# Two first loads and the end of VectorE's work tied in program order, and seven chunks of the last product held for its own PSUM banks

## The chip, the cores and the metric

The kernel runs on one core of one Trainium2 chip. The metric is the device time of one execution in microseconds (us), the median of several runs. Engines are named as in the profile: PE is TensorE's matmuls and PEld its weight loads, DVE is VectorE, ACT is ScalarE, POOL is GpSimd and SP is SyncE. A letter q behind an engine's name (SPq) stands for that engine's sequencer, which also issues DMAs.

## The reference

One layer of a decoder trunk on 256 tokens with 2048 features, all in float32. Only its last part is touched by the end of the change:

```python
h = rms_norm(x, norm_ffn_pre)
a, b = jnp.split(h @ w_up, 2, axis=-1)            # w_up: 2048 x 11264
c = conv_b + sum(conv_w[j] * shifted(a, j))       # width 3, causal
y = (gelu(c, approximate=True) * b) @ w_down      # w_down: 5632 x 2048
x = x + rms_norm(y, norm_ffn_post)                # out: 256 x 2048
```

Before it stand a norm, one combined projection `w_in`, two kinds of attention (latent and sliding-window), their output products, two sigmoid gates and `w_out`.

## The kernel before

**Weights.** Every weight comes from HBM in chunks of 128 rows by 1024 columns (512 KB, float32), by a DMA on SP's queue into a `raw` tile. `convert` (L157, L158) splits a chunk in two: ScalarE's CAST rounds it to `whi`, VectorE's subtraction leaves the rest in `wlo`. A product then takes three matmuls for each 128 x 512 piece, high by high, high by low and low by high (`mm3`, L189 to L191, or L500 for the first product), so one chunk with both halves of the tokens (t = 0 and t = 1, 128 tokens each) makes 12 matmuls of 512 columns. VectorE's and ScalarE's part of a chunk runs some chunks ahead of TensorE, as far as the rings of `raw` and `whi`/`wlo` tiles allow.

**Start.** SP loads `gx` and the `xr` tiles (the columns of x) and chunks of `w_in` in turn. The first product (L500 for the first four rows of chunks, L189 to L191 for the rest) has the banks `acckv` and `accq`. The chunk `raw_201` feeds 12 matmuls, then `raw_224`, `raw_245` and `raw_268` feed 12 each.

**Two tiles that are free from the start.** `raw_x` (tag `rx`, in the pool `base`) is one more raw tile that `new_raw` deals out in turns in the FFN's part; its first user is the chunk `raw_8782` of `w_up`. The staging tile of `park_sums` (tag `sg`; its loads are L234) takes two chunks of `w_down`; VectorE subtracts them from one another there (L238) and POOL's queue writes the results to DRAM (L243, L248), from where the seven-product steps below load them. Its first user is `tc_s`, in the middle of the attention. A scheduler places an instruction where it thinks that it can start; the first loads into these two tiles wait for nothing that was written before. `tc.keep_in_program_order` ties an instruction to its place among the others of its engine.

**The last product.** `w_down` is multiplied in column blocks of 1024. The last one, named `dc`, has the rows from 24 x 128 on and the columns from 1024 on. Its four PSUM banks are `cdc`: c[0] and c[1] for t = 0 (columns 1024 to 1535 and 1536 to 2047), c[2] and c[3] for t = 1. `pair_gemm` goes through the order "ppsspssppp": p (`plain`) is two chunks with 12 matmuls each; s (`seven_parked`) is two chunks' worth in seven products instead of eight, with parked sums and four more banks `qdc`. In the last six chunks only t = 0 is multiplied as they come (6 matmuls a chunk); the operands of t = 1 are kept in the list `held`, and are multiplied behind them (`rest`) into four new banks `zb`. So c[0] and c[1] are whole earlier, and the norm of t = 0 runs beside the matmuls of t = 1. The first of the held chunks is converted into two tiles of its own (`wh`), since the ring's would be reused.

**The end on VectorE.** `z_block` adds a bank to the sum so far (`ds`, L1387), ScalarE squares the result with a running sum, and VectorE multiplies by the gain `gpost` (L1390). `z_pre` (L1406 to L1408) gathers the sums of all but the last 256 columns; `finish` makes the scale `rz` (L1413 on ScalarE, L1414 to L1418 on VectorE), and its four `result` steps (L1422) make 512 columns of the output each, whose DMA (L1425) follows on SP's queue. Before, what c[2] and c[3] hold is added by L1478, what the banks `zb` hold by L1387 and L1489, and the last two `result` steps of t = 0 are kept behind the last `z_block` of t = 1.

**x2b.** The residual stream is loaded again for the last step by `unpark` (L1256, four DMAs of 256 KB for each t) into the memory of the token sums `sb`, so each of these loads waits until TensorE has read the last of those sums.

Of the kernel before, what the change touches and what calls it, by code (L numbers as in the profile page):

```python
# [11 lines left out]
F32 = mybir.dt.float32  # L12
F32R = mybir.dt.float32r
# [3 lines left out]
ALU = mybir.AluOpType  # L17
AX = mybir.AxisListType

P = 128  # L20
# [22 lines left out]
def trunk_layer(ctx, tc, x, x_cols_in, conv_cols_in, g_mix_post, g_ffn_post, w_in, w_q, w_kv,  # L43
                sinks, rel, wo_a, wo_b, w_out, w_up, w_down, rope_tab, strip_sel, out):
    nc = tc.nc
# [14 lines left out]
    def sb(pl, shape, name, dt=F32, tag=None, bufs=None):  # L60
        return pl.tile(shape, dt, name=name, tag=tag or name, **({"bufs": bufs} if bufs else {}))
# [55 lines left out]
    more_raw = []  # L117
# [10 lines left out]
    def wchunk(src, shape, own=None, rawp=None, rbufs=1, parts=None):  # L128
        i = cnt[0]
        cnt[0] += 1  # L130
        n = int(np.prod(shape))
        raw = rawp.tile([P, 1024], F32, name=f"raw{i}", tag="xraw", bufs=rbufs) if rawp else \
            new_raw(f"raw{i}")
        dst = raw[:, :n]
        if len(shape) == 2:
            dst = dst.rearrange("p (a b) -> p a b", a=shape[0])
        elif len(shape) == 3:
            dst = dst.rearrange("p (a b c) -> p a b c", a=shape[0], b=shape[1])
        if len(shape) == 3:
            for k in range(shape[0]):  # L140
                nc.sync.dma_start(dst[:, k], src[:, k])
        else:
            nc.sync.dma_start(dst, src)
        return convert(raw, n, own=own, parts=parts)

    def convert(raw, n, own=None, parts=None, into=None):
# [14 lines left out]
    def raw_row(src, n=1024):  # L161
        i = cnt[0]
        cnt[0] += 1
        raw = new_raw(f"raw{i}")
        nc.sync.dma_start(raw[:, :n], src)
        return raw

    steps = defaultdict(list)
# [19 lines left out]
    def mm3(o, ah, al, bh, bl, start, stop):  # L188
        pe.matmul(o, ah, bh, start=start, stop=False)  # L189
        pe.matmul(o, ah, bl, start=False, stop=False)  # L190
        pe.matmul(o, al, bh, start=False, stop=stop)  # L191
# [27 lines left out]
    def weight_sums(even, odd, ta, tb):  # L219
# [3 lines left out]
        vec.tensor_tensor(tb[:, a], odd[:, b], ta[:, a], op=ALU.subtract)  # L223
        vec.tensor_tensor(tb[:, b], odd[:, a], tb[:, a], op=ALU.subtract)

    def park_sums(name, w, k, c0, pl, tag, t0, bufs=None):

        td = [dram.tile([P, 1024], F32, name=f"{name}{i}") for i in range(2)]
        st = []

        def load():
            st.append(sb(pl, [P, D], f"{name}s", tag=tag, bufs=bufs))
            for i in range(2):
                pool.dma_start(st[0][:, i * 1024:(i + 1) * 1024], w[(k + i) * P:(k + i + 1) * P, c0:c0 + 1024])  # L234

        def less(o, x, y):
            o, x, y = (st[0][:, i * 512:(i + 1) * 512] for i in (o, x, y))
            tc.keep_in_program_order(vec.tensor_tensor(o, x, y, op=ALU.subtract))  # L238
# [12 lines left out]
        at(t0, even)  # L251
        at(t0 + 1, odd)
        return td
# [5 lines left out]
    def pair_gemm(name, w, k0, c0, order, act_of, s_of, kind, d, place=None, sums=None, parked=None, held=None, into=None):  # L259
# [13 lines left out]
        def plain(u, last):  # L273
            for k in (2 * u, 2 * u + 1):
                chunks[0] -= 1
                w_ = convert(raw_row(row(k)), 1024, into=into() if hold and chunks[0] == hold - 1 else None)
                for t in range(NT):
                    if t and chunks[0] < hold:
                        held[hold - 1 - chunks[0]] = (act_of(k, 1), w_)
                        continue  # L280
                    for j in range(2):
                        mul(c[2 * t + j], act_of(k, t), half(w_, j),
                            chunks[0] == (hold if t else 0) and (j == 1 or not left[0]))
                tick()

        def seven_parked(u, last):
            s1, s2, s3, s4 = s_of(u)
            if not q:
                q[:] = banks(1 - kind, f"q{name}_")
            q1, q5, q7, q6 = q  # L290
            w_ = convert(raw_row(row(2 * u + 1)), 1024)
            mul(c11, act_of(2 * u + 1, 0), half(w_, 0))
            mul(c12, s4, half(w_, 1))
            w_ = convert(raw_row(row(2 * u)[:, 0:512], 512), 512)
            mul(q1, act_of(2 * u, 0), half(w_, 0), last)
# [7 lines left out]
            mul(c21, act_of(2 * u + 1, 1), half(w_, 0), last and 0 < hold == chunks[0])  # L303
            tick()
            if last:
                end_sums()
# [1072 lines left out]

    ssz = [sb(p3, [P, NB], f"ssz{t}") for t in range(NT)]  # L1380

    def z_block(acc, b, t, later=None):
# [4 lines left out]
        vec.tensor_tensor(z, zo, acc[:, o:o + n], op=ALU.add)  # L1387
        jt = sb(p6, [P, 512], f"zj{b}_{t}", tag="jk", bufs=1)
        act.activation(jt[:, :n], z, AF.Square, accum_out=ssz[t][:, b:b + 1])
        scaled = lambda: vec.tensor_tensor(zo, z, gpost2[c0 // 1024][:, c0 % 1024:c0 % 1024 + n], op=ALU.mult)  # L1390
        if later is None:
            scaled()
        elif callable(later):
            later()
            scaled()
        else:
            at(later, scaled)
# [12 lines left out]
    def finish(t, late=()):  # L1410
# [6 lines left out]
        vec.scalar_tensor_tensor(w, v, y[:, 0:1], y, op0=ALU.mult, op1=ALU.mult)  # L1417
        vec.scalar_tensor_tensor(r, w, 1.5, y, op0=ALU.add, op1=ALU.mult)  # L1418

        def result(j):  # L1420
            a, b = 512 * j, 512 * j + 512
            ins = vec.scalar_tensor_tensor(dsum_all[t][:, a:b], dsum_all[t][:, a:b], r[:, 0:1], x2_all[t][:, a:b], op0=ALU.mult, op1=ALU.add)  # L1422
            if j in late:
                tc.keep_in_program_order(ins)
            nc.sync.dma_start(out[t * P:(t + 1) * P, a:b], dsum_all[t][:, a:b])  # L1425

        for j in range(4):
            if j not in late:
                result(j)
        return lambda: [result(j) for j in late]  # L1430
# [39 lines left out]
    c = pair_gemm("dc", w_down, 24, 1024, B2_ORDER, lambda k, t: (GH(k)[:, t * P:(t + 1) * P], GL(k)[:, t * P:(t + 1) * P]),  # L1470
                  lambda u: sb_of[u], 1, ud2_tiles, parked=parked_b2, held=held,
                  into=lambda: [sb(base, [P, 1024], f"wh{k}", F32R, tag=f"ahl{k}") for k in (6, 7)])
# [8 lines left out]
    def rest(o, todo, a, b):  # L1481
        o = o[:, a % 512:a % 512 + b - a]
        for i, (x_, (wh, wl)) in enumerate(todo):
            mm3(o, *x_, wh[:, a:b], wl[:, a:b], i == 0, i == len(todo) - 1)

    rest(part[0], held, 0, 512)
    z_block(part[0], 2, 1)
    rest(part[1], held[:-3], 512, 1024)
    vec.tensor_tensor(dsum[1][3], dsum[1][3], part[1], op=ALU.add)  # L1489
    for i in range(2):  # L1490
        rest(part[2 + i], held[-3:], 512 + i * 256, 768 + i * 256)
# [94 lines left out]
```

## Time and profile before

| what | us |
|---|---|
| median of 3 runs | 1464.42 (1462.93 to 1465.0) |
| the profiled execution | 1465.17 |
| its span, first to last instruction | 1463.2 |
| TensorE busy with matmuls | 1449.8 |
| VectorE busy | 1142.1 |
| ScalarE busy | 861.4 |

All times of instructions are microseconds from the start of the profiled execution's span; that execution took 1.97 us more than its span. A row of the timeline has the start, the time to the end of the last of its instructions, engine, line, operation, names of the tiles written and read, count, and in brackets the idle time before it with what ended it. A matmul's row shows its latency too (0.39 us at 512 columns); how often the array takes one is read from the distance of two starts.

### The profile page before, as it was taken

Reading aid. Unit: us, or ns where it says so; the run is one execution under the profiler, and the core shown is the slowest. Engines: PE = TensorE matmul, PEld = TensorE weight load, DVE = VectorE, ACT = ScalarE, POOL = GpSimd, SP = SyncE. Lnnn points to the kernel's source line nnn. Section 1 sums busy time; section 2 is a strip of 40 time slices with the busy share of each in tenths; the row PEclk is TensorE's granted clock in tenths of the full one; section 3 lists DMA queues with packets and bytes.
Section 4 is the critical chain, followed back from the end, with each engine's and each line's share of the span. In section 5 each row is a group of like instructions: output and inputs, shape, how many; then the busy total and the mean of one; then the engine's idle time right before and its main releaser. Section 6 shows DMA issues by size and latency. Waiting matters only on the chain.

```text
span 1463.2 us, 21340 instructions
## 1 busy us (share of the span) xinstructions
PE 1449.8 (99%) x7531; PEld 1236.5 (85%) x7531; DVE 1142.1 (78%) x1992; ACT 861.4 (59%) x1412; POOL 107.2 (7%) x192
## 2 busy tenths in 40 slices
PE   9999999999999999999999999999999999999997
PEld 7888888888888888888888888888888888888885
DVE  7688896765868765768799989776778797876798
ACT  6588875544555554446576665655646565665663
POOL 0021110010000101100000011000000100000000
PEclk9999999999999999999999999999999999999999
DMA  9756476698775779865666899756888888667875
GB/s 330 214 155 177 114 247 188 216 314 285 239 214 180 231 239 327 280 195 172 215 216 206 276 311 298 262 172 211 312 275 265 308 271 288 193 189 237 309 262 205
DMA packets 164199, 351.08 MB, mean 240 GB/s; under 512 B 20555, under 2 KB 31724, under 8 KB 164092
## 3 DMA queue, kind: packets, MB, share of 16 engines
q1 hardware_dynamic: 144480, 280.40, 59.3%
q0 software_dynamic: 19520, 69.27, 13.9%
q8 instruction: 59, 0.97, 0.3%
q14 instruction: 48, 0.39, 0.1%
q10 hardware_dynamic: 92, 0.05, 0.0%
HBM read 318.16 MB, written 31.51 MB: 239 GB/s over the span
## 4 chain that ended last, share of the span: by engine, by line
PE 93%; DVE 2%; DMA 2%; ACT 1%; issue 1%; DVEq 0%; SPq 0%; ACTq 0%
PE accg L189 11%; PE accg L191 11%; PE accg L190 11%; PE ua L1282 10%; PE ub L1282 10%; PE ub L1286 5%; PE ua L1286 5%; PE cd L190 2%; PE cd L191 2%; PE cd L189 2%; DMA raw<-in_ffn_w_down_dram 1%; DVE wlo L158 1%; PE mpo L966 1%; PE cg L190 1%; PE cg L189 1%; PE cw L191 1%
## 5 line engine op out<-in xcount | busy, mean ns | idle before, releaser
L158 DVE TENSOR_TENSOR wlo<-raw,whi 128x1024 fp32r<-128x1024 f32 (+2 forms) x499 | 589.0, 1190 | 213.3 <-ACT whi L157 204.5
L157 ACT CAST whi<-raw 128x1024 fp32r<-128x1024 f32 (+2 forms) x499 | 508.3, 1026 | 397.9 <-PE accg L191 153.2
L189 PE MATMUL accg<-whi,ahl 128*128 128x512 f32 (+1 forms) x416 | 162.8, 391 | 0.0
L191 PE MATMUL accg<-whi,ahl 128*128 128x512 f32 (+1 forms) x416 | 160.6, 386 | 0.0
L190 PE MATMUL accg<-wlo,ahl 128*128 128x512 f32 (+1 forms) x416 | 159.8, 384 | 0.0
L1282 PE MATMUL ub<-ahl,whi 128*128 128x512 f32 x640 | 154.6, 391 | 0.0
L1282 PE MATMUL ua<-ahl,whi 128*128 128x512 f32 x640 | 154.6, 391 | 0.0
L1282 PEld LDWEIGHTS ua<-ahl,whi 128*128 128x128 f32 x640 | 117.5, 188 | 22.7
L1282 PEld LDWEIGHTS ub<-ahl,whi 128*128 128x128 f32 x640 | 117.5, 188 | 22.6
L189 PE MATMUL accg<-whi,bhl 128*128 128x512 f32 x320 | 125.6, 393 | 0.0
L191 PE MATMUL accg<-whi,bhl 128*128 128x512 f32 x320 | 124.8, 390 | 0.0
L190 PE MATMUL accg<-wlo,bhl 128*128 128x512 f32 x320 | 124.7, 390 | 0.0
L191 PEld LDWEIGHTS accg<-whi,ahl 128*128 128x128 f32 x416 | 78.1, 188 | 15.5
L190 PEld LDWEIGHTS accg<-wlo,ahl 128*128 128x128 f32 x416 | 78.2, 188 | 13.1
L189 PEld LDWEIGHTS accg<-whi,ahl 128*128 128x128 f32 x416 | 78.2, 188 | 12.9
L1286 PEld LDWEIGHTS ub<-ahl,wlo 128*128 128x128 f32 x640 | 82.2, 191 | 3.2
L1286 PEld LDWEIGHTS ua<-ahl,wlo 128*128 128x128 f32 x640 | 82.2, 191 | 3.1
L1286 PE MATMUL ua<-ahl,wlo 128*128 128x256 f32 x640 | 83.7, 283 | 0.0
L1286 PE MATMUL ub<-ahl,wlo 128*128 128x256 f32 x640 | 83.3, 283 | 0.0
L191 PEld LDWEIGHTS accg<-whi,bhl 128*128 128x128 f32 x320 | 60.1, 188 | 12.6
L189 PEld LDWEIGHTS accg<-whi,bhl 128*128 128x128 f32 x320 | 60.1, 188 | 12.1
L190 PEld LDWEIGHTS accg<-wlo,bhl 128*128 128x128 f32 x320 | 60.1, 188 | 12.1
(624 smaller groups left out, 2535.9 us busy)
## 6 DMA issues: line engine op xcount, KB each, us to landing
raw<-in_ffn_w_up_dram SPq DMA_DIRECT2D x142, 512.0 KB, 4.7
raw<-in_w_in_dram SPq DMA_DIRECT2D x105, 512.0 KB, 4.6
raw<-in_ffn_w_down_dram SPq DMA_DIRECT2D x66, 512.0 KB, 5.5
xraw<-in_ffn_w_up_dram SPq DMA_DIRECT2D x34, 512.0 KB, 5.5
raw<-in_w_o_swa_dram SPq DMA_DIRECT2D x32, 512.0 KB, 5.0
raw<-in_w_o_mla_dram SPq DMA_DIRECT2D x32, 512.0 KB, 5.2
raw<-in_w_out_dram SPq DMA_DIRECT2D x26, 512.0 KB, 4.4
ta_s<-in_ffn_w_down_dram POOLq DMA_DIRECT2D x24, 512.0 KB, 6.0
```

The lines of the kernel that those rows point to most:

```text
L157: act.copy(hi[:, a:b], raw[:, a:b])
L158: vec.tensor_tensor(lo[:, a:b], raw[:, a:b], hi[:, a:b].bitcast(F32), op=ALU.subtract)
L189: pe.matmul(o, ah, bh, start=start, stop=False)
L190: pe.matmul(o, ah, bl, start=False, stop=False)
L191: pe.matmul(o, al, bh, start=False, stop=stop)
L966: pe.matmul(o, w(t), p_[:, c], start=n == 0, stop=n == 5)
L1282: pe.matmul(acc[i], hi[:, c], hn[p][:, j * 512:(j + 1) * 512], start=p + j == 0, stop=stop)
L1286: pe.matmul(acc[i][:, 0:256], lo[:, c], hn[p][:, j * 512:j * 512 + 256], start=False, stop=False)
```

## The change

Four edits go together.

First, the first load into the tile `rx` is kept in program order on SP's queue (in `wchunk` or `raw_row`, whichever comes first), and the first two loads into the staging tile are kept in program order on POOL's.

Second, seven chunks are held instead of six. The seventh from the end is the second chunk of the third p, ahead of two s steps; it is converted into two tiles of its own, `wfa` and `wfb` (tag `f`), by a new `held_into`. The one after it keeps `wh`.

Third, the held matmuls of t = 1 go on in c[2] and c[3] themselves (`more=True`: the bank isn't started anew), but for the last three chunks' share of the last 512 columns, which keeps two banks `zb` of 256 columns each. The two additions L1478 and the two of the banks `zb` become one for c[2] (in `z_block`) and one for c[3].

Fourth, VectorE's order at the end: `finish(0, 2)` makes two results of t = 0, then the addition of c[2] is kept in its place, then come the other two results of t = 0, then the addition of c[3], kept in its place too, and then the two blocks of 256 columns.

```diff
+            ins = nc.sync.dma_start(dst, src)
+            if more_raw and more_raw[-1] is raw_x and "rx" not in staged:
+                staged.add("rx")
+                tc.keep_in_program_order(ins)
...
-                pool.dma_start(st[0][:, i * 1024:(i + 1) * 1024], w[(k + i) * P:(k + i + 1) * P, c0:c0 + 1024])
+                ins = pool.dma_start(st[0][:, i * 1024:(i + 1) * 1024], w[(k + i) * P:(k + i + 1) * P, c0:c0 + 1024])
+                if tag not in staged:
+                    tc.keep_in_program_order(ins)
+            staged.add(tag)
...
-    held = [None] * 6
+    held = [None] * 7
...
+    def held_into(left):
+        if left == 6:
+            return [sb(p6, [P, 1024], f"wf{n}", F32R, tag="f" + n, bufs=2) for n in "ab"]
+        if left == 5:
+            return [sb(base, [P, 1024], f"wh{k}", F32R, tag=f"ahl{k}") for k in (6, 7)]
...
-    for j in range(2):
-        vec.tensor_tensor(dsum[1][2 + j], dsum[1][2 + j], c[2 + j], op=ALU.add)
-    part = [pacc.tile([P, 512], F32, name=f"zb{i}", tag="acc") for i in range(4)]
+    part = [pacc.tile([P, 512], F32, name=f"zb{i}", tag="acc") for i in range(2)]
...
-    rest(part[0], held, 0, 512)
-    z_block(part[0], 2, 1)
-    rest(part[1], held[:-3], 512, 1024)
-    vec.tensor_tensor(dsum[1][3], dsum[1][3], part[1], op=ALU.add)
+    rest(c[2], held, 0, 512, True)
+    rest(c[3], held[:-3], 512, 1024, True)
...
-    rest_of_0 = finish(0, (2, 3))
-    z_block(part[2], 3, 1)
+    result_of_0 = finish(0, 2)
+    z_block(c[2], 2, 1, tied=True)
+    for j in (2, 3):
+        result_of_0(j)
+    tc.keep_in_program_order(vec.tensor_tensor(dsum[1][3], dsum[1][3], c[3], op=ALU.add))
+    z_block(part[0], 3, 1)
     z_pre(1)
-    z_block(part[3], 4, 1, rest_of_0)
+    z_block(part[1], 4, 1)
     finish(1)
```

How instructions stand on the engines is shown at three places. On SP's queue at the start of the program there stood before (`raw_8782` is the chunk of `w_up` in the tile `rx`):

```order
L421 DMA xr_128<-in_x_cols_dram 128x256
L143 DMA raw_201<-in_w_in_dram 128x2x512
L421 DMA xr_129<-in_x_cols_dram 128x256
L143 DMA raw_8782<-in_ffn_w_up_dram 128x2x512
L143 DMA raw_224<-in_w_in_dram 128x2x512
L421 DMA xr_130<-in_x_cols_dram 128x256
L143 DMA raw_245<-in_w_in_dram 128x2x512
```

and there stands now:

```order
L432 DMA xr_128<-in_x_cols_dram 128x256
L143 DMA raw_201<-in_w_in_dram 128x2x512
L432 DMA xr_129<-in_x_cols_dram 128x256
L143 DMA raw_224<-in_w_in_dram 128x2x512
L432 DMA xr_130<-in_x_cols_dram 128x256
L143 DMA raw_245<-in_w_in_dram 128x2x512
```

The load of `raw_8782` has left the start; it now stands behind that of `raw_8760`, its neighbour in the FFN. On POOL's queue the two loads of `tc_s` have moved from the row behind the copy of `gmat`, near the start, to the row ahead of their own write-back in the attention, behind the writes of `yb_d`. Elsewhere up to the last product no engine's order differs.

On SP's queue at the end of the program there stood before:

```order
L165 DMA raw_14270<-in_ffn_w_down_dram 128x1024
L165 DMA raw_14286<-in_ffn_w_down_dram 128x1024
L165 DMA raw_14303<-in_ffn_w_down_dram 128x1024
L1256 DMA x2b_14250<-x_d 128x512 x4
L165 DMA raw_14315<-in_ffn_w_down_dram 128x1024
L1425 DMA out_dram<-ds_7715 128x512 x4
```

and there stands now (the chunks are the same ones, with numbers 6 lower):

```order
L168 DMA raw_14264<-in_ffn_w_down_dram 128x1024
L168 DMA raw_14280<-in_ffn_w_down_dram 128x1024
L1267 DMA x2b_14244<-x_d 128x512 x4
L168 DMA raw_14297<-in_ffn_w_down_dram 128x1024
L168 DMA raw_14309<-in_ffn_w_down_dram 128x1024
L1433 DMA out_dram<-ds_7715 128x512 x4
```

Both of the last two chunks, not only the last, now stand behind the four loads of `x2b` for t = 1.

On VectorE at the end there stood before (`ds_7715` is t = 0, `ds_7716` is t = 1):

```order
L1417 SCALAR_TENSOR_TENSOR wz_14402<-vz_14400,yz_14401 128x1
L1489 TENSOR_TENSOR ds_7716<-ds_7716,zb_14347 128x512
L1390 TENSOR_TENSOR ds_7716<-ds_7716,gpost_1_13437 128x512
L1418 SCALAR_TENSOR_TENSOR rz_14403<-wz_14402,yz_14401 128x1
L1387 TENSOR_TENSOR z_1_14413<-ds_7716,zb_14348 128x256
L1422 SCALAR_TENSOR_TENSOR ds_7715<-ds_7715,rz_14403,x2b_14121 128x512 x2
L1390 TENSOR_TENSOR ds_7716<-z_1_14413,gpost_1_13437 128x256
L1406 TENSOR_REDUCE zpre_13434<-ssz_13432 128x1
L1387 TENSOR_TENSOR z_1_14421<-ds_7716,zb_14349 128x256
L1407 TENSOR_SCALAR zpre_13434<-zpre_13434 128x1
L1422 SCALAR_TENSOR_TENSOR ds_7715<-ds_7715,rz_14403,x2b_14121 128x512
```

and there stands now:

```order
L1427 SCALAR_TENSOR_TENSOR wz_14393<-vz_14391,yz_14392 128x1
L1428 SCALAR_TENSOR_TENSOR rz_14394<-wz_14393,yz_14392 128x1
L1432 SCALAR_TENSOR_TENSOR ds_7715<-ds_7715,rz_14394,x2b_14121 128x512 x2
L1398 TENSOR_TENSOR ds_7716<-ds_7716,cdc_13919 128x512
L1432 SCALAR_TENSOR_TENSOR ds_7715<-ds_7715,rz_14394,x2b_14121 128x512 x2
L1403 TENSOR_TENSOR ds_7716<-ds_7716,gpost_1_13437 128x512
L1506 TENSOR_TENSOR ds_7716<-ds_7716,cdc_13920 128x512
L1398 TENSOR_TENSOR z_1_14413<-ds_7716,zb_14338 128x256
L1398 TENSOR_TENSOR z_1_14421<-ds_7716,zb_14339 128x256
L1403 TENSOR_TENSOR ds_7716<-z_1_14413,gpost_1_13437 128x256
L1416 TENSOR_REDUCE zpre_13434<-ssz_13432 128x1
```

All four results of t = 0 now stand ahead of the last two blocks of t = 1; before, two stood among and behind them. Further up on VectorE, the additions L1474 and L352 of the seven products now stand ahead of the conversion of `raw_14249`, the fifth chunk from the end, where they stood behind it.

More of the change, by code (lines that the diff above doesn't have):

```diff
@@ L164, in raw_row @@
         raw = new_raw(f"raw{i}")
-        nc.sync.dma_start(raw[:, :n], src)
+        ins = nc.sync.dma_start(raw[:, :n], src)
+        if more_raw and more_raw[-1] is raw_x and "rx" not in staged:
+            staged.add("rx")
+            tc.keep_in_program_order(ins)
         return raw
@@ L275, in plain @@
                 chunks[0] -= 1
-                w_ = convert(raw_row(row(k)), 1024, into=into() if hold and chunks[0] == hold - 1 else None)
+                w_ = convert(raw_row(row(k)), 1024, into=into(chunks[0]) if hold else None)
                 for t in range(NT):
@@ L282, in plain @@
                         mul(c[2 * t + j], act_of(k, t), half(w_, j),
-                            chunks[0] == (hold if t else 0) and (j == 1 or not left[0]))
+                            not (chunks[0] or (t and hold)) and (j == 1 or not left[0]))
                 tick()
@@ L302, in seven_parked @@
             mul(q6, s2, half(w_, 1), last)
-            mul(c21, act_of(2 * u + 1, 1), half(w_, 0), last and 0 < hold == chunks[0])
+            mul(c21, act_of(2 * u + 1, 1), half(w_, 0))
             tick()
@@ L1380, in trunk_layer, with z_block @@
     ssz = [sb(p3, [P, NB], f"ssz{t}") for t in range(NT)]
-    def z_block(acc, b, t, later=None):
+    def z_block(acc, b, t, later=None, tied=False):
         c0, n = blocks[b]
@@ L1421, in result @@
             a, b = 512 * j, 512 * j + 512
-            ins = vec.scalar_tensor_tensor(dsum_all[t][:, a:b], dsum_all[t][:, a:b], r[:, 0:1], x2_all[t][:, a:b], op0=ALU.mult, op1=ALU.add)
-            if j in late:
-                tc.keep_in_program_order(ins)
+            vec.scalar_tensor_tensor(dsum_all[t][:, a:b], dsum_all[t][:, a:b], r[:, 0:1], x2_all[t][:, a:b], op0=ALU.mult, op1=ALU.add)
             nc.sync.dma_start(out[t * P:(t + 1) * P, a:b], dsum_all[t][:, a:b])
[L1427 to L1430, printed above, removed]
+        for j in range(n):
+            result(j)
+        return result
     a_tile = lambda name, k: sb(base, [P, 1024], name, tag=f"ahl{k}")
```

20 lines of the change are left out of this document (10 added, 10 removed).

## The prediction

> **What bounds the kernel now.** First the page: the busy times, then the chain that ended last.
>
> ```profile
> PE 1449.8 (99%) x7531; PEld 1236.5 (85%) x7531; DVE 1142.1 (78%) x1992; ACT 861.4 (59%) x1412; POOL 107.2 (7%) x192
> PE 93%; DVE 2%; DMA 2%; ACT 1%; issue 1%; DVEq 0%; SPq 0%; ACTq 0%
> ```
>
> TensorE is the bound, and the change takes no matmul away (7340 rows on that engine in both programs). So it can only win where TensorE stands or runs slowly, and behind its last matmul. The change touches the start and the end, so I cut both into stretches. The start, with TensorE's timeline:
>
> ```profile
> 13.00:14.70 1.70, 0.04 (x1) 0.00 (x0) 0.02 (x1) 1.09 (x2) 0.00 (x0) 1.00 1.06 407
> 16.40:19.80 3.40, 3.40 (x10) 2.62 (x9) 3.33 (x5) 3.33 (x8) 0.00 (x0) 0.50 1.03 390
> 19.80:22.30 2.50, 2.50 (x13) 2.02 (x12) 1.95 (x4) 2.42 (x4) 0.00 (x0) 1.00 1.05 402
> ...
> 8.01 1.81 PE L500 MATMUL accq<-whi,ahl 128*128 128x512 f32 x4
> 10.13 1.08 PE L500 MATMUL acckv<-whi,ahl 128*128 128x512 f32 x4
> 14.71 1.19 PE L500 MATMUL acckv<-whi,ahl 128*128 128x512 f32 x4 [1.67 <-ACT whi L157]
> 15.96 0.87 PE L500 MATMUL acckv<-wlo,ahl 128*128 128x512 f32 x2
> 22.26 0.39 PE L189 MATMUL acckv<-whi,ahl 128*128 128x512 f32 x1
> 24.98 0.39 PE L189 MATMUL acckv<-whi,ahl 128*128 128x512 f32 x1
> ```
>
> TensorE stands from 13.0 to 14.7 for the high half of `raw_224`, then for its low half until 15.96. From 16.4 to 19.8 its granted clock is 0.50. From 22.26 to 24.98 it makes the 12 matmuls of `raw_268`, one every 0.227 us (2.72 us a chunk), and goes on so without a gap. Why `raw_224` is late:
>
> ```profile
> 5.99 0.38 SPq L143 DMA_DIRECT2D raw<-in_w_in_dram  x1
> 13.61 1.05 ACT L157 CAST whi<-raw 128x1024 fp32r<-128x1024 f32 x1 [4.47 <-DMA raw<-in_w_in_dram]
> q1 hardware_dynamic: 751, 1.25, 57.1%
> q0 software_dynamic: 288, 1.05, 45.3%
> raw<-in_ffn_w_up_dram SPq DMA_DIRECT2D x1, 512.0 KB, 8.6
> 3.34 1.21 POOL L234 DMA_DIRECT2D tc_s<-in_ffn_w_down_dram  x2
> raw<-in_w_in_dram SPq DMA_DIRECT2D x105, 512.0 KB, 4.6
> DMA to landing us min/median/max: 3.4/7.5/8.8
> ```
>
> The load is issued at 5.99 and needs 7.6 us. The two queue rows are for 6 to 12.5 us: the transfer engines are full, and 1.05 MB of the 2.30 MB is POOL's queue, which holds only `tc_s` there. On SP's queue the 0.52 MB of `w_up` stand ahead of `raw_224`. `tc_s` is first read at 380 us, the `w_up` chunk at 855 us (rows below). So 1.57 MB that nobody needs yet pass in front of what TensorE waits for: at the 390 to 407 GB/s of the stretches above 3.9 to 4.0 us of transfer.
>
> **First edit, the two ties.** Without those bytes `raw_224` needs at most the 4.6 us that is the median of such loads: it lands by 10.6 instead of 13.6. (The last row is for the loads of the first 30 us: at their shortest, 3.4, it lands at 9.4.) I add what stood behind it, the CAST of 1.05 us and a subtraction of 1.23 us: high half at 11.7, low half at 13.0. TensorE, busy with `raw_201` since 10.13, ends its 12 matmuls at 10.13 + 12 x 0.227 = 12.85, and wants the low half four matmuls later, at 13.76. So there is no gap, and with no gap I expect no stretch at half clock. `raw_268` then starts at 12.85 + 2 x 2.72 = 18.29 instead of 22.26: **3.97 us earlier**. Whether the rest follows:
>
> ```profile
> 25.31 1.22 DVE L158 TENSOR_TENSOR wlo<-raw,whi 128x1024 fp32r<-128x1024 f32 x1
> 27.84 1.22 DVE L158 TENSOR_TENSOR wlo<-raw,whi 128x1024 fp32r<-128x1024 f32 x1
> 25.00:30.00 5.00, 5.00 (x24) 4.14 (x23) 5.00 (x9) 4.96 (x9) 0.00 (x0) 1.00 1.01 374
> ```
>
> VectorE is full there, but takes 27.84 - 25.31 = 2.53 us a chunk, TensorE 2.72; and the bytes of a chunk with its columns of x, 0.52 + 0.13 MB, take 1.7 us at 390 GB/s. Both start 3 us earlier than before, so their lead over TensorE grows, and I take the 3.97 whole. From there to the last product TensorE carries the chain, so the gain is kept.
>
> What the moved loads cost where they go:
>
> ```profile
> 353.14 1.14 POOL L793 DMA_DIRECT2D yb_d<-tb  x2 [12.33 <-DVE tb L792]
> 380.43 1.41 DVE L238 TENSOR_TENSOR tc_s<-tc_s 128x512 f32<-128x512 f32 x2
> DMA to landing us min/median/max: 2.9/4.6/8.4
> 855.45 1.22 DVE L158 TENSOR_TENSOR wlo<-raw,whi 128x1024 fp32r<-128x1024 f32 x1
> 839.11 7.05 SPq L143 DMA_DIRECT2D raw<-in_ffn_w_up_dram  x3
> 355.00:360.00 5.00, 5.00 (x24) 4.14 (x23) 2.04 (x2) 2.11 (x2) 0.00 (x0) 1.00 0.82 288
> ```
>
> `tc_s` is issued behind `yb_d`, by 355.4, and even at 8.4 us (the longest for this tile, third row) is there 16 us ahead of 380.4. Behind it in POOL's queue stands only its own write-back. `raw_8782` is issued behind `raw_8760`, the second of the three issues from 839, so by 846, and is converted at 855.45: 9 us for a load of about 6. TensorE is full beside the first (24 matmuls in 5.00 us); the loads beside each tie come up to 2.7 or 1.3 us later (1.05 and 0.52 MB at 390 GB/s), and the chunks that wait converted ahead of TensorE hide that. I take 0; at worst, if all of it showed, 2.7 + 1.3 us would come back.
>
> **Second and third edit, the held chunk.** The six matmuls of the seventh chunk (1.36 us) leave a place where TensorE had no gap and go behind the last six chunks, where its wait for data is this:
>
> ```profile
> PEld cdc L190 <- DVE wlo L158: 1.1, 3, 0.5
> 1431.00:1435.00 4.00, 4.00 (x19) 3.31 (x18) 3.44 (x3) 3.43 (x4) 0.00 (x0) 1.00 1.02 398
> 1431.56 2.40 DVE L158 TENSOR_TENSOR wlo<-raw,whi 128x1024 fp32r<-128x1024 f32 x2 [1.11 <-ACT whi L157]
> 1433.52 0.39 PE L190 MATMUL qdc<-wlo,sb 128*128 128x512 f32 x1
> 1443.52 2.35 DVE L158 TENSOR_TENSOR wlo<-raw,whi 128x1024 fp32r<-128x1024 f32 x2
> 1439.00:1445.50 6.50, 6.42 (x27) 4.70 (x27) 6.50 (x9) 1.09 (x2) 0.00 (x0) 1.00 0.42 158
> 1435.53 1.75 SPq L1256 DMA_DIRECT2D x2b<-x_d  x4
> 1442.52 1.06 ACT L157 CAST whi<-raw 128x1024 fp32r<-128x1024 f32 x1 [3.48 <-DMA raw<-in_ffn_w_down_dram]
> ```
>
> At most those 1.1 us can be won. But the transfers are full (398 GB/s) up to 1435, so data doesn't come sooner because TensorE does: the low half that it uses at 1433.52 is ready at 1432.8 (the first of two conversions from 1431.56), and at 1433.52 - 1.36 = 1432.16 it would stand 0.6 us for it. Then two additions (0.60 each) precede a conversion that they followed: another 0.5. Then VectorE is the limit (6.50 of 6.50 us busy from 1439 on) with the same five conversions and eight additions to make, so the last low half, ready at 1445.87 (the end of the two from 1443.52), comes at most 0.2 earlier. The six matmuls fill a gap only to open one. The two last loads behind `x2b` are no limit by my sum: TensorE reads the last `sb` 1.36 - 0.6 = 0.7 us sooner, `x2b` is issued from 1434.8, the two chunks behind it at 1436.6 and 1437.0, and they land by about 1442, while VectorE comes to them at 1443.3.
>
> **Third and fourth, VectorE's end.**
>
> ```profile
> 1446.98 0.68 DVE L1387 TENSOR_TENSOR ds<-ds,cdc 128x512 f32<-128x512 f32 x1
> 1450.67 0.22 DVE L1417 SCALAR_TENSOR_TENSOR wz<-vz,yz 128x1 f32<-128x1 f32 x1
> 1454.61 0.41 DVE L1387 TENSOR_TENSOR z<-ds,zb 128x256 f32<-128x256 f32 x1
> 1457.47 2.74 DVE L1422 SCALAR_TENSOR_TENSOR ds<-ds,rz,x2b 128x512 f32<-128x512 f32 x4
> ```
>
> The addition of c[0] starts at 1446.98; now I get 1446.8 (the last low half at 1445.7, three matmuls of 0.227 and a latency of 0.39). From there to the scale of t = 0 the order is old, less two additions: its step at 1450.67 stood 3.69 behind c[0], a result follows it and one more step of 0.22, less some 0.3 for the addition that held the chain up: 3.8 us. Then two results (1.32), c[2] (0.60), two results (1.32), a gain (0.60), c[3] (0.60), and two blocks of 256 (0.33 each): the second block starts 8.6 us behind c[0], at 1455.4, where 1454.61 stood. From it to the four results took 2.86, with two results of 0.66 of t = 0 among it; without these, ScalarE's second square, root and the small steps remain, 2.25. So the results start at 1457.65 instead of 1457.47: **0.2 us later**. Two additions are saved (1.2 us), but VectorE spends them waiting for c[0]. I keep 1.2 us either way.
>
> **The sum** is 1465.17 - 3.97 + 0.2 = 1461.4 against the profiled execution, which lies 0.75 above the median of the three runs (1464.42); carried to that median, **1460.7**.
>
> **The rivals.** (1) *The half clock stays.* I take 16.4 to 19.8 for the echo of the gap at 13.0 to 14.7. If it is not, the 12 matmuls of `raw_245` lose 3.4/2 = 1.7 us again: 1462.4. For it: the gap is only half as long as the slow stretch. Against it: before 16.4 the clock is 1.00, after 19.8 again 1.00, and nothing else but that gap precedes it. [...] (2) *The end wins after all:* the two saved additions count in full, 1.2 us, since the gaps ahead of c[0] close: 1459.2. (3) *The early loads are not the limit:* if `raw_224` landed at 12.2 all the same, since SP's queue alone moved only 1.25 MB in those 6.5 us, half the standing and maybe the slow clock stay: 1462.6. Against it: the same queue moves 402 GB/s from 19.8 on. (4) *Slower:* the two last chunks hang behind `x2b`. From the first `x2b` issue to the last CAST were 7.0 us (1435.53 to 1442.52), with one more chunk about 8.3, and its CAST and subtraction add 2.3. So the last low half comes 10.6 us behind that issue, and the 3.8 us won are gone when it comes past 1445.87 + 3.8 = 1449.7, with `x2b` released later than 1439.1, 4.3 behind my 1434.8: when TensorE stands that long ahead of its last read of `sb`. At 1440 the time is 1465.3. Against it: ahead of that read I find only the 0.6 us above. That a tie wouldn't move its load is ruled out by the order.
>
> **How the numbers follow.** Forecast 0.66, rival (1) 0.12, (2) 0.12, (3) 0.06, (4) 0.04. A measurement of this kernel tells about 0.2% (2.9 us) from no change, so "faster" ends at 1461.5. The forecast with its 1.2 us at the end lies on the good side with five sixths, 0.56, rival (2) wholly: faster 0.68; rivals (1) and (3) and the rest: same 0.28; slower 0.04. The range reaches to rivals (1) to (3) with what the unknown ends add, and to 0.7 below (2), since without gaps the start hangs on when the clock rises (four matmuls took 1.81 us at 8.01, 1.08 at 10.13): 1458.5 to 1463.0.
>
> **What would show it.** Right: no packets of POOL's queue before 30 us; the CAST of `raw_224` before 11.7; no wait of TensorE between 10 and 25 us, and no stretch at 0.50 there; its first L195 matmul near 18.3. The end: TensorE's last matmul near 1449.6 instead of 1453.4, and the last four results from 1453.7 on. Wrong: a wait for `tc_s` or the `w_up` chunk near 380 or 855, a slow stretch at 16 to 20 without a gap, or ScalarE still waiting for the two last chunks at 1439.

## The result and the profile after

| | before | changed |
|---|---|---|
| median of 22 runs, us | 1464.87 | 1462.12 |
| ratio, 95% interval | | 0.9983 (0.9976 to 0.9990) |
| the profiled execution, us | 1465.17 | 1462.8 |
| its span, us | 1463.2 | 1460.7 |
| the chunk `raw_268` starts on TensorE | 22.26 | 17.81 |
| matmul 7100 of 7531, counted from 0, starts (ahead of the new end, same code) | 1355.98 | 1352.68 |
| the last four results start | 1457.47 | 1454.97 |

The change wins 2.75 us by the medians, 2.5 us by the two spans. The table cuts that in three: the start wins 4.45, the way to matmul 7100 gives back 1.15, the end gives back 0.80. This is one trace against one; how far they scatter is told with the experiments.

The start, in the stretches of before and TensorE's and ScalarE's timelines (a row has start, time, engine, line, operation, tiles, count, and in brackets the wait before it):

```profile
PE 1446.6 (99%) x7531; PEld 1234.8 (85%) x7531; DVE 1141.7 (78%) x1990; ACT 859.0 (59%) x1412; POOL 107.2 (7%) x192
13.00:16.40 3.40, 3.40 (x16) 2.82 (x16) 2.81 (x4) 3.05 (x7) 0.00 (x0) 1.00 0.98 336
16.40:19.80 3.40, 3.40 (x16) 2.81 (x16) 2.78 (x6) 3.25 (x7) 0.00 (x0) 1.00 1.05 406
q1 hardware_dynamic: 1117, 1.85, 92.1%
10.29 1.05 ACT L160 CAST whi<-raw 128x1024 fp32r<-128x1024 f32 x1 [1.30 <-DMA raw<-in_w_in_dram]
12.37 1.07 PE L511 MATMUL acckv<-whi,ahl 128*128 128x512 f32 x4
17.81 0.39 PE L195 MATMUL acckv<-whi,ahl 128*128 128x512 f32 x1
349.99 1.07 POOL L242 DMA_DIRECT2D tc_s<-in_ffn_w_down_dram  x2
376.14 1.41 DVE L249 TENSOR_TENSOR tc_s<-tc_s 128x512 f32<-128x512 f32 x2
```

Between 6 and 12.5 us only SP's queue moves data (fourth row; POOL's has none before 30 us). The CAST of `raw_224` comes at 10.29 instead of 13.61, its matmuls follow at 12.37 without a bracket, the granted clock stays 1.00 where it was 0.50, and `raw_268` starts at 17.81. The staging tile's loads are issued at 350 and its first subtraction, at 376.14, waits for nothing.

The end: TensorE's list of waits, then ScalarE, VectorE and SP:

```profile
PE qdc L196 <- DVE wlo L161: 0.8, 1, 0.8
PE x2T L1103 <- DVE x L1100: 0.7, 1, 0.7
PE qdc L195 <- ACT whi L160: 0.2, 1, 0.2
PE cdc L196 <- DVE wlo L161: 0.2, 1, 0.2
1427.19 1.05 ACT L160 CAST whi<-raw 128x1024 fp32r<-128x1024 f32 x1 [2.45 <-DMA raw<-tc]
1428.27 2.51 DVE L161 TENSOR_TENSOR wlo<-raw,whi 128x1024 fp32r<-128x1024 f32 x2 [2.19 <-ACT whi L160]
1440.27 2.49 DVE L161 TENSOR_TENSOR wlo<-raw,whi 128x1024 fp32r<-128x1024 f32 x2
1443.83 0.69 DVE L1398 TENSOR_TENSOR ds<-ds,cdc 128x512 f32<-128x512 f32 x1 [1.06 <-PE cdc L197]
1454.97 2.74 DVE L1432 SCALAR_TENSOR_TENSOR ds<-ds,rz,x2b 128x512 f32<-128x512 f32 x4
raw<-tc SPq DMA_DIRECT2D x2, 512.0 KB, 8.4
```

TensorE, which had no wait worth a row in the end of before, now waits 1.2 us for the last s step and the chunk behind it. Behind that stands ScalarE, 2.45 us idle for a parked chunk (`raw` from `tc`), and behind that the transfer: the two last parked loads take 8.4 us from issue to landing (last row, for issues from 1415 to 1422). From 1428.27 to 1442.76 VectorE has no gap worth a row, then it waits 1.06 us for the last matmuls of c[0]. Two of the signs that the prediction named for the end failed by about a microsecond: TensorE's last matmul ends at 1450.70 instead of 1449.6, and the last four results start at 1454.97 instead of 1453.7.

### The profile page after: what moved, and what is told of

Its sections match the earlier page's. It is cut to its first block, busy times and chain, and to the rows that moved or that the text cites. A ratio compares the mean times of both kernels' runs of the same rounds, so it can differ in the third digit from the quotient of the medians.

```text
span 1460.7 us, 21344 instructions
## 1 busy us (share of the span) xinstructions
PE 1446.6 (99%) x7531; PEld 1234.8 (85%) x7531; DVE 1141.7 (78%) x1990; ACT 859.0 (59%) x1412; POOL 107.2 (7%) x192
## 4 chain that ended last, share of the span: by engine, by line
PE 93%; DVE 3%; DMA 2%; ACT 1%; issue 1%; POOL 0%; DVEq 0%; ACTq 0%; POOLq 0%
PE accg L195 10%; PE accg L197 10%; PE accg L196 10%; PE ua L1293 10%; PE ub L1293 10%; PE ub L1297 5%; PE ua L1297 5%; PE cd L196 2%; PE cd L195 2%; PE cd L197 2%; DVE wlo L161 1%; PE mpo L977 1%; PE cdb L196 1%; PE cdb L195 1%; PE cdb L197 1%; PE cw L195 1%
```

## The experiments

Theory, after this reading: the ties win what the forecast says, and the new end costs about 1.5 us, because its data come no sooner than TensorE, now six matmuls ahead, wants them. Rivals: the start's gain is lost on the way whatever the end does; VectorE's order, not the data, holds the end; and for the start, the half clock has another cause than the gap. Ratios are to before, on the same chip.

**The changed kernel once more** (`e0_again`).

> The changed kernel once more, for a second trace of it. If the waits of 0.7 us for x at 740 us (shift from -4.26 to -3.3) and of 0.2 and 0.8 us for the parked halves at 1428 to 1430 belong to the change, they are there again and the ratio to before is 0.9983. If the one at 740 is scatter, it is gone or elsewhere, and TensorE is some 4.2 us ahead of before until 1400 us.

Measured: 0.9986 (0.9977 to 0.9995). Its profiled execution took 1466.67 us, 5 above its own median of 1461.61, with waits at several places:

```profile
PE cdb L196 <- DVE wlo L161: 0.8, 1, 0.8
PE qdc L196 <- DVE wlo L161: 0.8, 1, 0.8
PE qdc L195 <- ACT whi L160: 0.5, 1, 0.5
PE cdc L195 <- ACT whi L160: 0.6, 1, 0.6
PE cdc L196 <- DVE wlo L161: 0.6, 2, 0.4
PE ub L1293 <- DVE uu L1192: 0.3, 1, 0.3
1430.34 1.05 ACT L160 CAST whi<-raw 128x1024 fp32r<-128x1024 f32 x1 [3.42 <-DMA raw<-tc]
1443.26 1.05 ACT L160 CAST whi<-raw 128x1024 fp32r<-128x1024 f32 x1 [5.53 <-DMA raw<-in_ffn_w_down_dram]
1444.34 2.50 DVE L161 TENSOR_TENSOR wlo<-raw,whi 128x1024 fp32r<-128x1024 f32 x2 [1.00 <-ACT whi L160]
1447.87 0.69 DVE L1398 TENSOR_TENSOR ds<-ds,cdc 128x512 f32<-128x512 f32 x1 [1.04 <-PE cdc L197]
```

The wait for the last s step is there again, so it belongs to the change. The end is 3.66 us longer than in the first trace: matmul 7100 starts at 1353.06 and the last results at 1459.01, which is 105.95 us, against 102.29. Of this 1.7 us are lost within 40 matmuls behind matmul 7100, where the code is that of before; the rest stands in later waits for data. The first parked half is cast 77.3 us behind matmul 7100 (74.5 in the first trace), and VectorE stands 1.00 us for the last two chunks, which stand behind `x2b` of t = 1 (the rows of ScalarE and VectorE at 1443.26 and 1444.34). Two of the eleven executions were this slow (1466.17 and 1466.67); the other nine took 1460.45 to 1463.12. The waits on the way move about: at 740 us this trace lost 0.3 (0.96 in the first), at 806 us 0.7 (0 in the first), and `e1_ties` below, whose code there is the same, nothing. Cut at twelve places between 30 us and matmul 7100, the other stretches agree within 0.2 us over all fourteen traces, but for 0.4 at 255 us. So of the 1.15 us given back on the way some 1.0 is scatter of one execution. One difference goes with a tie: the hundred matmuls from some 447 us on take 17.16 to 17.21 us in all ten traces with the staging tie, 17.07 to 17.11 in the four without.

**The two halves of the change apart** (`e1_ties`: before with the first edit alone; `e2_tail`: before with the other three). These lines are in the one and not in the other:

```diff
+            ins = nc.sync.dma_start(dst, src)
+            if more_raw and more_raw[-1] is raw_x and "rx" not in staged:
+                staged.add("rx")
+                tc.keep_in_program_order(ins)
...
+                ins = pool.dma_start(st[0][:, i * 1024:(i + 1) * 1024], w[(k + i) * P:(k + i + 1) * P, c0:c0 + 1024])
+                if tag not in staged:
+                    tc.keep_in_program_order(ins)
```

> Before with the two ties alone. Theory (the start is worth the whole 4.4 us that its trace shows, and the new end gives about 1.5 back): 1464.9 - 4.4 = 1460.5, ratio 0.9970, no half clock at 16 to 20 us, no wait at 1428 to 1434. Rival (what the start wins is lost on the way whatever stands at the end): 1462.4, the time of the whole change.

> Before with the second to fourth edit alone, without the ties. Theory (the new end costs 1.5 us, as TensorE's matmuls fall from 4.0 to 2.5 us ahead of before between 1428 and 1435): 1466.4, ratio 1.0010, with the half clock at 16 to 20 us still there. The forecast's own term (+0.2): 1465.1. The rival that the two saved additions count (-1.2): 1463.7.

Measured: the ties alone 0.9976 (0.9968 to 0.9985), 1460.55 against 1464.15; the rest alone 1.0015 (1.0006 to 1.0023), 1466.69. So the new end costs time, and the ties alone beat the whole change: 1460.55 against 1461.61 on the same chip. The rest alone costs 2.54 us by the medians, more than the 1.5 of the theory; its single trace is 1.50 later than that of before at `raw_268` (23.76), where the code is the same, and 0.74 longer at the end. The rival that the gain is lost on the way falls. In the trace of the ties alone TensorE has no wait behind the start, and the same rows as above read:

```profile
1425.77 1.05 ACT L160 CAST whi<-raw 128x1024 fp32r<-128x1024 f32 x1 [0.84 <-DMA raw<-tc]
1426.85 2.55 DVE L161 TENSOR_TENSOR wlo<-raw,whi 128x1024 fp32r<-128x1024 f32 x2 [1.20 <-ACT whi L160]
1438.94 2.35 DVE L161 TENSOR_TENSOR wlo<-raw,whi 128x1024 fp32r<-128x1024 f32 x2
1442.41 0.68 DVE L1398 TENSOR_TENSOR ds<-ds,cdc 128x512 f32<-128x512 f32 x1
1452.90 2.74 DVE L1433 SCALAR_TENSOR_TENSOR ds<-ds,rz,x2b 128x512 f32<-128x512 f32 x4
raw<-tc SPq DMA_DIRECT2D x2, 512.0 KB, 7.6
```

Counted from matmul 7100 (1352.18 here, 1352.68 in the changed kernel), the first parked half is cast at 73.6 against 74.5, the last low half is ready at 89.1 against 90.1, c[0] is added at 90.2 against 91.15, and from there to the last results it takes 10.49 against 11.14. The end is 1.57 us longer (100.72 against 102.29). All traces together say what of this is firm. The five with the old end and `x2b` in its old place (before, the ties alone and the next three runs) take 100.7 to 101.5, before itself 101.49; the three with the new end take 102.29, 105.95 and 102.23. From c[0] to the last results it is 10.45 to 10.49 in the five and 11.14, 11.14 and 11.50 in the three: this part is firm. The first parked half is cast at 73.2 to 74.5 in the five (74.5 in before) and at 74.5, 77.3 and 73.9 in the three. So the 0.9 us between the two traces above can be scatter, as the changed kernel has this half no later than before has it; TensorE only wants it sooner.

**Which bytes at the start count** (`e3_staging_tie`: the staging tile's tie alone, 1.05 MB of POOL's queue gone; `e4_raw_tie`: the raw chunk's alone, 0.52 MB of SP's queue gone).

> Before with the tie of the staging tile alone: 1.05 MB of POOL's queue leave the start, the 0.52 MB of w_up stay ahead of the late chunk. Theory 1 (bytes count, whichever queue has them): the chunk lands 2.6 us earlier, near 11.0, no gap of TensorE, no half clock: nearly the whole gain of the two ties, 1464.2 - 4 = 1460.2. Theory 2 (what stands ahead in SP's own queue counts): lands 1 us earlier at most, a gap stays, 1463 or more.

> Before with the tie of the extra raw chunk alone: 0.52 MB of SP's queue leave the start, the 1.05 MB of POOL's stay. Theory 1 (bytes count): the chunk lands 1.3 us earlier, near 12.3, a gap of 0.5 and one of 0.4 us stay in place of 1.67 and 0.4. If a gap that short still lowers the clock, 1464.2 - 1.2 = 1463.0; if not, 1464.2 - 2.9 = 1461.3. Theory 2 (SP's own queue counts): lands before 11, no gap, 1460.2.

Measured: 0.9977 (0.9968 to 0.9986) and 0.9985 (0.9976 to 0.9993). The rows of the chunk's CAST and first matmuls, of the staging tie and then of the raw tie with its clock:

```profile
10.98 1.05 ACT L157 CAST whi<-raw 128x1024 fp32r<-128x1024 f32 x1 [1.94 <-DMA raw<-in_w_in_dram]
13.45 1.07 PE L505 MATMUL acckv<-whi,ahl 128*128 128x512 f32 x4
```

```profile
12.67 1.04 ACT L160 CAST whi<-raw 128x1024 fp32r<-128x1024 f32 x1 [3.30 <-DMA raw<-in_w_in_dram]
13.77 1.21 PE L508 MATMUL acckv<-whi,ahl 128*128 128x512 f32 x4 [0.94 <-ACT whi L160]
16.40:19.80 3.40, 3.40 (x17) 2.81 (x16) 3.09 (x6) 3.40 (x7) 0.00 (x0) 1.00 1.05 399
```

The chunk is 2.6 us earlier without the 1.05 MB and 0.9 without the 0.52 MB, where the sum by bytes said 2.6 and 1.3. One trace tells this only to about a microsecond: where the loads at the start are those of before, the CAST stands at 13.61 (before), 14.33 (`e5_fill`) and 15.13 (`e2_tail`); in the ten traces with the staging tie it stands at 9.43 to 10.98. Within that, the bytes count on either queue: 2.6 us for 1.05 MB of POOL's, 0.9 us for 0.52 MB of SP's. The staging tie alone is as good as both within the interval. With the raw tie alone a gap of 0.94 us stays, but no half clock.

**The gap filled** (`e5_fill`: before, with small matmuls of the warm-up kind ahead of the late chunk's; their bank is read by nobody).

```diff
+            if k == 2:
+                fill = pss.tile([P, 512], F32, name="fill", tag="s")
+                for i in range(FILL):
+                    tc.keep_in_program_order(pe.matmul(fill[:, 0:P], ramp, ramp, start=True, stop=True))
             product(k, acc_kv, w[1])
...
+FILL = 28
```

> Before with 28 small matmuls of ramp into a bank that nobody reads, ahead of the late chunk's matmuls; loads are as before, so the chunk comes as late, but TensorE has something to do in some 1.6 us of the gap. Theory (the gap lowers the clock): granted clock 1.00 from 16 to 20 us, 1464.2 - 1.7 = 1462.5. Rival (the half clock has another cause, such as the load of the transfers or the change of work at 16): the stretch at 0.50 stays, 1464.2.

Measured: 0.9996 (0.9987 to 1.0005); that holds both the 1.7 us of the theory (0.9988) and nothing, so the time doesn't decide. The trace does:

```profile
13.43 1.74 PE L531 MATMUL fill<-ramp 128*128 128x128 bf16 x28
15.42 1.20 PE L500 MATMUL acckv<-whi,ahl 128*128 128x512 f32 x4 [0.26 <-ACT whi L157]
16.40:19.80 3.40, 3.34 (x15) 2.58 (x15) 3.29 (x6) 3.29 (x7) 0.00 (x0) 1.00 1.06 395
```

The chunk comes even later than in before (15.42 against 14.71), yet the clock stays 1.00, and from the chunk's first matmul to `raw_268` it is 5.94 us (21.36 - 15.42) against 7.55 (22.26 - 14.71): the 1.6 us of the half clock are gone. As the chunk came 0.7 us later, `raw_268` gains only 0.9 us of this, which fits the 0.66 between the medians (1464.68 and 1464.02). So the gap, not the work or the transfers behind it, lowered the clock: the 1.67 us of before did it, the 0.26 us that are left here did not.

**Six chunks held** (`e6_hold6`: the changed kernel, but `held = [None] * 6` and no tiles `wfa`, `wfb`).

> The changed kernel with six chunks held in place of seven (ties, own banks and VectorE's order as in the change). Theory (the seventh held chunk takes 1.36 us of TensorE's work out from in front of a place that waits for data): no wait of TensorE over 0.3 us at 1428 to 1434; c[0] as with the ties alone or 0.2 earlier (1442.2), from there 11.1 us to the last results as in the changed kernel's trace, against 10.5 in that of the ties alone: 1460.6 + 0.4 = 1461.0. Rival (own banks and order are what costs): 1462.3, as the changed kernel.

Measured: 0.9977 (0.9968 to 0.9987), 1461.43. TensorE's list has no wait behind the start, and:

```profile
1441.69 0.69 DVE L1398 TENSOR_TENSOR ds<-ds,cdc 128x512 f32<-128x512 f32 x1 [0.85 <-PE cdc L197]
1452.92 2.74 DVE L1432 SCALAR_TENSOR_TENSOR ds<-ds,rz,x2b 128x512 f32<-128x512 f32 x4
```

From matmul 7100 (1351.84) c[0] comes at 89.85, sooner than in the three traces with seven held (91.15, 94.81 and 90.73), and the last results 11.23 later, as with seven. So the seventh chunk is what makes TensorE wait, and c[0] is late with it, though by how much one trace can't say: the old end has c[0] at 90.2 to 91.0. Own banks with VectorE's new order cost 0.65 to 1.0 behind c[0], where the old end takes 10.49. Against the ties alone this end is 0.36 us longer in the traces (101.08), not told apart by the times.

**Where the data wait** (`e7_x2b_last`: the changed kernel with all eight `x2b` loads tied behind the last chunk's; `e10_x2b_t0_late`: those of t = 0 five steps later, between the chunks behind the parked ones; `e8_ties_x2b`: `x2b` last with the ties and the old end). The diff is that of `x2b` last, where `True` ties each load; for t = 0 alone, (8, 14) became (13, 14) and nothing is tied.

```diff
-    for i in range(8):
-        at(now[0] + (8, 14)[i // 4] + i % 4, lambda i=i: unpark(i // 4, i % 4))
...
                   into=held_into)
+    for i in range(8):
+        unpark(i // 4, i % 4, True)
```

> The changed kernel with all eight loads of x2b tied behind the last chunk's load. Theory (the loads of x2b for t = 0 pass ahead of the last two parked chunks and delay them while the transfers are full, then those for t = 1 delay the last two chunks): TensorE's waits of 1.0 us at 1428 to 1430 are gone, c[0] is added about 1 us earlier, 1462.4 - 1.2 = 1461.2. Rival (VectorE's queue is the limit from 1428 on, data or not): 1462.4, c[0] no earlier. Slower than 1462.4 if x2b lands behind the scale of t = 0 (20 us behind its issue, at 1447.6).

> The changed kernel with the four loads of x2b for t = 0 asked for five steps later, so that they stand between the loads behind the two parked chunks; those for t = 1 stay ahead of the last two chunks. Theory (it is t = 0's loads ahead of the parked chunks that make TensorE wait at 1428 to 1430): that wait is gone; the last two chunks still come behind x2b of t = 1, and c[0] is about 1 us earlier: 1461.4. Rival (the last two chunks behind t = 1's loads are what costs): 1462.2, c[0] as in the changed kernel.

> Before with the two ties, and all eight loads of x2b tied behind the last chunk's load; six chunks held and the old banks and VectorE order. Theory (transfers ahead of the last parked chunks are what the end waits for, with either order of VectorE): c[0] some 0.8 us earlier than with the ties alone, 1459.7. Rival (with six chunks held the data are early enough, VectorE is the limit): 1460.5, as with the ties alone; then the end of the changed kernel with x2b last, 1460.0 on the same terms, is the better one.

Measured: 0.9974 (0.9964 to 0.9984), 0.9988 (0.9979 to 0.9997) and 0.9972 (0.9961 to 0.9982). With `x2b` last:

```profile
raw<-tc SPq DMA_DIRECT2D x2, 512.0 KB, 5.3
1423.18 1.05 ACT L160 CAST whi<-raw 128x1024 fp32r<-128x1024 f32 x1 [0.27 <-DMA raw<-tc]
PE cdc L196 <- DVE wlo L161: 1.6, 1, 1.6
1437.24 1.89 DVE L1474 TENSOR_TENSOR ds<-ds,ue 128x512 f32<-128x512 f32 x3
1439.05 1.22 DVE L161 TENSOR_TENSOR wlo<-raw,whi 128x1024 fp32r<-128x1024 f32 x1
```

The parked loads take 5.3 us instead of 8.4, their first half is cast 4 us earlier (3.6 counted from matmul 7100), and TensorE's waits for the last s step are gone: `x2b` ahead of them was what made them late. The rival then takes over as the next limit: TensorE waits 1.6 us for one low half whose subtraction, at 1439.05, stands behind three additions that VectorE makes first. c[0] still comes 2.3 us sooner from matmul 7100 (88.8). With only t = 0's loads moved the theory's 1461.4 is missed, the median is 1462.82:

```profile
PE cdc L196 <- DVE wlo L161: 2.0, 3, 0.7
PE cdc L196 <- DVE wh L161: 0.6, 1, 0.6
1445.60 0.69 DVE L1398 TENSOR_TENSOR ds<-ds,cdc 128x512 f32<-128x512 f32 x1 [2.20 <-PE cdc L197]
```

The wait for the s step is gone, but four new ones of 0.6 to 0.7 us come with the chunks that `x2b` now stands ahead of. This trace is that of its slowest execution (1464.52; the fastest took 1460.50), so the sizes are an upper end. Of the three places tried for this megabyte, two have chunks behind them, and TensorE waited for such chunks in both; behind the last chunk there is none to wait for. With the old end, `x2b` last brings nothing that can be measured against the ties alone (0.9972 and 0.9976): there the data were early enough, and TensorE waits 1.4 us behind the same three additions.

**VectorE relieved** (`e9_pool_sums`: as with `x2b` last, and the four additions of `ue` to `ds` on GpSimd; `e11_pool_sums_six`: the same two steps with the ties and the old end).

```diff
-... vec.tensor_tensor(dsum[t][2 + j], dsum[t][2 + j], ud2[i], op=ALU.add))
+... pool.tensor_tensor(dsum[t][2 + j], dsum[t][2 + j], ud2[i], op=ALU.add))
```

> The changed kernel with x2b last and the four additions of ue to ds on GpSimd instead of VectorE. Theory (with the data early VectorE's order is the limit: in the trace with x2b last TensorE waits 1.6 us for a low half behind three of these additions): the wait goes, c[0] 1.5 us earlier, 1460.0 - 1.3 = 1458.7. Rival (GpSimd's additions take so long that c[0] or c[2] waits for ds, 0.95 us for half the size in the changed kernel's trace): 1460 or more.

> The two ties, x2b last, the four additions on GpSimd, but the end otherwise as before (six held chunks, four banks, old order). Against the same with seven held: if the new end is worth anything once neither data nor these additions stand in its way, this one is slower by the two additions it saves, up to 1.2 us (1459.9 against 1458.7); if it isn't, they are equal within 0.5 us.

Measured: 0.9961 (0.9947 to 0.9976), 1459.31, the best of all; and 0.9974 (0.9965 to 0.9984), 1460.98.

```profile
1434.75 5.79 POOL L1474 TENSOR_TENSOR ds<-ds,ue 128x512 f32<-128x512 f32 x3 [1.76 <-DVE ue L353]
1439.03 0.69 DVE L1400 TENSOR_TENSOR ds<-ds,cdc 128x512 f32<-128x512 f32 x1 [0.89 <-PE cdc L197]
1440.57 0.75 DVE L1400 TENSOR_TENSOR z<-ds,cdc 128x256 f32<-128x256 f32 x2 [0.86 <-POOL ds L1474]
PE cdc L196 <- DVE wlo L161: 0.7, 1, 0.7
```

c[0] comes 1.2 us sooner still (87.6 from matmul 7100), but an addition takes GpSimd 1.9 us, VectorE waits 0.86 for the second, and from c[0] to the last results it is 12.8. From matmul 7100 to them the two ends take 100.37 and 100.53. The intervals of the two ratios overlap, but on this chip all five executions with seven held (1458.73 to 1459.67) lie below all ten with six (1460.13 to 1462.56). So the times favour the new end by 1.7 us once neither data nor these additions stand in its way, where up to 1.2 was expected. The two traces differ by 0.16 at the end, so what makes the 1.7 isn't shown.

## Why the prediction was right, and which term was off

*The ties.* The mechanism held at each step: the bytes, the earlier CAST, no gap, no half clock, no wait where the loads went. The size too: 3.97 us forecast, 4.45 between two traces, 3.6 by the medians of the ties alone (1464.15 to 1460.55). `raw_268` was forecast at 18.29; ten traces without the gap have it between 17.55 and 19.16. Part of the 4.45 is luck of the pair, as the last section works out. Rival (1), a half clock that stays, is refuted by these traces, and another cause for it by the one with the gap filled; rival (3), loads that are not the limit, by the two ties apart.

*The way.* "So the gain is kept": right but for scatter. The two moved loads were costed at 0 and cost below 0.1 us together.

*The end.* This is the term that was mis-sized: +0.2 forecast; +0.80 between the traces of before and of the change, +1.57 from that of the ties alone, 1.06 between the medians of these two on one chip.

The step that failed in every trace is the chain behind c[0]: forecast 10.85 us to the last results, measured 11.14 twice and 11.50, against 10.49 of before. The forecast had seen the sign and half of the size.

The other step is the last low half, which was to come "at most 0.2 earlier". That "data doesn't come sooner because TensorE does" held: counted from matmul 7100 the first parked half is cast at 74.5 in before and in the changed kernel, VectorE is full from there on, and the last low half is ready at 89.9 and 90.1. But the forecast took these loads as if they came at a fixed time and VectorE as the only limit. The loads come behind `x2b` of t = 0 and take 8.4 us in the changed kernel, 7.6 with the ties alone and 5.3 with `x2b` moved away, and in the second trace of the changed kernel they came 2.8 us later than in the first (counted from matmul 7100; 1.7 of it are the loss right behind that). I had looked only at `x2b` of t = 1 and the two chunks behind it, as rival (4); the same mechanism struck one step earlier, on t = 0's.

Rival (4) itself wasn't far. In the first trace its point was not reached: moved back by the 3.3 us that the end began earlier, the last low half was ready at 1446.1, and the point was 1449.7. In the second it was: ready at 1446.83, it is moved back by 2.92 us to 1449.75, with VectorE waiting 1.00 us for the two chunks. The trace of the new end alone has 0.31 us of this wait. Why the parked loads take longer with seven held than with six stays open: the bytes ahead of them are the same, but the two chunks stand both ahead of `x2b`, which no run undid by itself.

*Two steps of the end held.* The two saved additions win nothing: the last low half and c[0] are 1.06 us apart in the changed kernel, which is the wait that they had filled. Rival (2), an end that wins 1.2, is refuted for this kernel by the run of the new end alone (1.0015).

*The sum.* 1465.17 - 4.45 + 1.15 + 0.80 = 1462.67; the profiled execution took 1462.8. The forecast was 3.77 below its base (3.97 less 0.2), the medians differ by 2.75; most of the difference is the end, the rest the start (3.6 by the medians instead of 3.97). Another 0.45 between the forecast of 1460.7 and the measured 1462.12 is the base, 1464.42 by three runs and 1464.87 by 22. So the median lies 0.6 above the 1461.5 at which the forecast let "faster" end: it had given that side 0.68, and the side where the time fell 0.28.

## What to carry to other kernels

Two loads that wait for nothing had gone to the start, where TensorE waited 1.67 us behind their bytes: look there for loads that are first read hundreds of microseconds later. When matmuls are taken out in front of a place that waits for data, ask what stands ahead of those data in the queue first: in the changed kernel the wait moved to TensorE (1.2 us). Here moving the other loads behind the last chunk brought back what the new end had lost (0.9974, against 0.9976 for the ties alone). Then look for the next limit at once; here it was VectorE's order, a wait of 1.6 us. And read a term of a microsecond from several traces: two of the same kernel differed by 3.7 us at the end.

## What the runs showed of the hardware

In the trace of before the records of the granted clock read 1.00 from 9.57 us, 0.50 from 16.40 and 1.00 again from 19.82: the slow one lasts 3.41 us. In the 3.41 us ahead of it, from 12.99 on, TensorE is idle for 1.74. In the trace of the new end alone it waits 2.13 us for the same chunk, until 16.23, and the rows from 16.40 to 19.80 and from 19.80 to 23.20 have a mean clock of 0.70 and 0.80. Where it waited less, the rows of the wait and behind it read 1.00: 0.95 us in the changed kernel (of the 3.41 from 1427.90 on), 1.31 us in its second trace (of the 5 from 1430 on), 0.94 us with the raw tie alone, 1.6 us with `x2b` last. So these waits cost their own length only. Where the line lies the traces don't tell, as the end of TensorE's work shows. In the trace of the ties alone it is idle there for 1.79 us of 3.42, and the next 3.40, wholly idle, still stand at 1.00 (the first number is the length, the second TensorE's busy time, the clock is the third from the end):

```profile
1447.18:1450.60 3.42, 1.63 (x14) 1.42 (x12) 3.42 (x11) 0.57 (x3) 0.00 (x0) 1.00 0.21 76
1450.60:1454.00 3.40, 0.00 (x0) 0.00 (x0) 3.29 (x10) 0.74 (x3) 0.00 (x0) 1.00 0.63 234
```

So 1.79 us kept the clock and 1.74 lost it: idle time as the profile has it, with modelled ends of the matmuls, doesn't decide alone.

The first record of the clock stands at 7.96 us in the changed kernel's trace and at 9.57 in that of before. In the changed kernel's the four matmuls from 5.78 on take 2.06 us, the four from 8.25 on 1.09. The ten traces without the gap have `raw_268` from 17.55 to 19.16, 1.6 us of scatter from run to run. Some 0.6 us of the 4.45 above is of this kind, by an estimate from two of them: `raw_268` starts at 17.81 in the changed kernel, and at 18.89 with the staging tie alone, where the two matmuls from 9.83 on still take 1.04 us and only the four from 10.68 on 1.11. With the clock risen at 9.57, between 7.96 and 10.68, it would have started near 18.4.
